# A two-layer hybrid decoder on one core: the order of paired weight loads, the planner's urgency rule, fixed buffers for the residual rows, and the queue that stores one product's tiles

## The chip, the core and the metric

The kernel runs on one core of a Trainium2 chip. Times are device microseconds of one execution. The core's engines are TensorE (PE, matmuls; PEld are its weight loads), VectorE (DVE), ScalarE (ACT), GpSimd (POOL) and SyncE (SP, which only issues DMA transfers here). ACT and POOL can issue DMA transfers too, each from its own queue, in the order of the program. The comparison is of the median time of the kernel before with that of the changed kernel.

## What is computed

Two layers, each with one input projection, three groups of heads, a gate and one output projection. Cut to what matters:

```python
def hybrid_layer(x, mem, w_in, b_forget, w_mem_kv, w_out, ln_gain, ln_bias):
    h = jnp.einsum('bsd,dn->bsn', x, w_in)
    (fq, fk, fv, fg, f_logit, dq, dk, dv, dg, iq, ik, iw, mq, mg) = jnp.split(h, offsets, axis=-1)
    y_fox = fox_attention(...) * silu(fg)       # 6 heads, causal, with a forget bias
    y_dsa = dsa_attention(...) * silu(dg)       # 6 heads, each query on its best 128 keys
    y_mem = memory_attention(...) * silu(mg)    # 4 heads on 256 memory tokens
    y = jnp.einsum('bsn,nd->bsd', jnp.concatenate([y_fox, y_dsa, y_mem], -1), w_out)
    return layer_norm(ALPHA * x + y, ln_gain, ln_bias)
```

The sequence has 512 rows, the model 2048 columns, a head 128; all inputs are float32. Every float32 operand is split into a high part (`whi`, `xh`, `qh`) and a low part (`wlo`, `xl`, `ql`), and a product is three matmuls: high x high, high x low, low x high.

## The kernel before

**Weights.** `stream()` lists the weights as chunks of 128 x 2048 float32 (1 MB), each worked on in two halves. The large projections are computed in blocks with seven products instead of eight (`P1`, `P7`, `Q4`, `P2`, `Q6`, `Q5`, `Q3`), so some right operands are sums of two weight blocks. Some of these sums are made in DRAM (by POOL, `weight_sums`), some by an accumulating load (`grow_w`) or on VectorE (`make_w`), and the operand T3 of P7 in pairs 1 to 5 is of the kind "pair": both blocks are loaded, one into `raw` and one, in four pieces of 256 KB, into slots called `other`, and `pair_w` adds them on VectorE. A layer has 10 such chunks.

For half n, the loop loads chunk i + 2 (`load_w`, on SP's queue), splits half n + 3 (ScalarE copies the high part, VectorE subtracts for the low part), adds the pair of half n + 4, and then issues the 12 matmuls of half n. `raw` has 7 buffers, the split weights (`whi`, `wlo`) 4, and nearly everything else, `other`, `z`, `row`, `vraw` and `halves` too, shares one pool of 69 slots.

**Stages of a layer.** Memory keys and values, then the indexer's chunks (iq), then the value products (`vs`: P1, P7, P2, Q6, Q4 for six pairs of column blocks, with early chunks for queries and keys between them), then Q5 and Q3 of the six pairs, during which the attention heads run, then the output projection.

**Side work.** What does not belong to a chunk is a generator. `begin(gen, wait)` puts it on a list, and `tick()` moves each on by a step; a yielded number is the count of ticks until its next step. A generator started with whole=True is moved twice a chunk in the indexer and once a chunk in the value products. `residual_rows` is one of them. In layer 1 it turns the normalised rows that layer 0 left in DRAM (x1) into layer 1's residual: for 12 tiles of 128 x 512 it loads the tile, multiplies by the gain and adds the bias (two VectorE operations; gain and bias rows are loaded by `load_row`, L1454), and stores the tile back from POOL's queue; the loads are on SP's queue (L1518). It takes a new slot for every tile and row. Its last step for a tile waits for `idle_dve(1.5)`: the planned VectorE at most 1.5 us behind TensorE.

**The planner.** While the kernel is written out, `Clock` keeps an estimated time for PE, ACT, DVE and POOL, charged for every operation. The heads are flows: generators that yield the engine of their next step. After each group of matmuls `advance()` picks, among the flows whose step `fits()`, the one with the lowest age, so the order in every engine's queue is fixed by it. Splits for Q5 and Q3 are flows as well (`split_steps`), with a due time of DUE = 10 us after they begin; one that is due within URGENT = 5 us goes ahead of all others, and `finish_flow` forces it out when its half is reached. An ACT or DVE step fits only if that engine is planned less than 1.5 us (heads) or 4 us (before) behind.

**Stores.** `val_out` takes a finished product out of PSUM. P2 of pair 0 is copied by ScalarE and stored with `store_v` (DMA `v<-vraw`); P2 of the pairs 1 to 5 is copied by ScalarE with its 16-bit halves interleaved (`halves`) and stored with `store_turned` (`vt<-halves`). Each is stored a tick later, two tiles a pair, from POOL's queue, as are all others of these stores. POOL's queue also holds the sums of weights, each behind a small operation (`seen<-mark`) that waits for ScalarE or VectorE.

Of the kernel before, what the change touches and what calls it, by code (L numbers as in the profile page):

```python
# [16 lines left out]
ALU = mybir.AluOpType  # L17
AX = mybir.AxisListType

P = 128  # L20
DM = 2048
# [15 lines left out]
SOON, LATER, URGENT, DUE = 1.5, 4.0, 5.0, 10.0  # L37
# [220 lines left out]
def kernel(  # L258
# [13 lines left out]
    clock = Clock()  # L272
    nc = Engines(tc.nc, clock)
# [11 lines left out]
    def uid(name):  # L285
        count[0] += 1
        return f"{name}_{count[0]}"
# [3 lines left out]
    def slot(name, dt=F32, w=512):  # L291
        t = slots.tile([P, w], dt, tag="s", name=uid(name))
        if name in COUNTED:
            out_now.append(t)
        return t
# [56 lines left out]
    def half(src, h):  # L352
        return src[:, h * H:(h + 1) * H]

    def load_w(i, pieces=2, some=(0, 1)):
        if i < len(chunks) and chunks[i][4][0] != "grown":
            kind, key = chunks[i][4]
            src = {"wall": lambda: wall[key], "sum": lambda: sums[key],
                   "pair": lambda: wall[key[0]]}[kind]()
            if chunks[i][0] == "out" and chunks[i][2][0] == "P7":  # L360
                for h in some:
                    t = [slot("grown") for _ in range(2)]
                    raw.setdefault(i, []).append(t)
                    for c in range(2):
                        nc.sync.dma_start(t[c], half(src, h)[:, c * 512:(c + 1) * 512])
                return
            w = DM // pieces
            for c in range(pieces):
                if c * 2 // pieces not in some:
                    continue  # L370
                if c * 2 % pieces == 0:
                    raw.setdefault(i, []).append(raws.tile([P, H], F32, tag="raw", name=uid("raw")))
                nc.sync.dma_start(raw[i][-1][:, c * w % H:c * w % H + w], src[:, c * w:(c + 1) * w])
                if i < 3 and c * 2 % pieces == 0:
                    load_mem(2 * i + c * 2 // pieces)
                if kind == "pair":
                    for e in (2 * c, 2 * c + 1):
                        t = others[i, e] = slot("other")
                        nc.sync.dma_start(t, wall[key[1]][:, e * 512:(e + 1) * 512])

    others = {}

    def pair_w(n):

# [220 lines left out]
    x1_d = dram.tile([SEQ, DM], F32, name="x1")  # L605
# [7 lines left out]
    def begin(gen, wait=0, last=False, whole=False, but=None):  # L613


        active.append([wait, gen, last, whole, but])
# [29 lines left out]
    def step_flow(f):  # L646

        eng = f[2]
        clock.floor = f[0]
        banks["held"] += f[3]  # L650
        try:
            need = next(f[1])
        except StopIteration:
            flows.remove(f)
            need = None
        clock.floor = 0.0
        done = clock.at[eng] + ahead[eng] if eng else clock.at["PE"]
        if need:
            f[2], f[3], floor, f[4] = (*need, None, None, None)[:4]
            f[3] = f[3] or 0  # L660
            f[0] = max(done, floor or 0.0)
# [14 lines left out]
    def advance():  # L676

        while flows:
            t = clock.at["PE"]
            freed[:] = [x for x in freed if x > t]  # L680
            room = 8 - banks["main"] - banks["held"] - len(freed)
            some = [f for f in flows if fits(f, room)]
            if not some:
                return
            step_flow(min(some, key=lambda f: f[5] if f[6] > t + URGENT else -1.0))

    def drain(done):

# [594 lines left out]
    def val_out(name, pair, st, ps):  # L1283

        j = 2 * pair
        m1, m7 = ("M1", pair, st), ("M7", pair, st)
        if name == "P2" and j in ROWS:
            d = slot("vraw")
            nc.scalar.activation(d, ps, AF.Copy)
            begin(store_v(d, (j, st)), 1)  # L1290
        elif name in ("P1", "P7"):
            d = vraw[m1 if name == "P1" else m7] = slot("vraw")
            nc.scalar.activation(d, ps, AF.Copy)
        elif name == "P2":
            begin(store_turned(halves(ps), (j, st)), 1)
        elif name == "Q6":
            d, e = slot("vraw"), vraw.pop(m7)
            nc.vector.scalar_tensor_tensor(d, ps, -1.0, vraw[m1], op0=ALU.mult,
                                           op1=ALU.subtract)
            nc.vector.tensor_tensor(e, e, d, op=ALU.add)  # L1300
            begin(store_v(d, (j + 1, 2 + st)), 1)
            begin(store_v(e, (j + 1, st)), 1)
        elif name == "Q4":
            d = vraw.pop(m1)
            nc.vector.tensor_tensor(d, d, ps, op=ALU.add)
            begin((store_v if j in ROWS else store_sum)(d, (j, 2 + st)), 1)
        elif j + 1 in ROWS:
            d = slot("vraw")
            nc.scalar.activation(d, ps, AF.Copy)
            begin(store_v(d, (j + 1, st + 2 * (name == "Q5")), True), 1)  # L1310
        else:
            d = vraw.pop(("base", name, pair, st))
            nc.vector.tensor_tensor(d, d, ps, op=ALU.add)
            begin(store_sum(d, (j + 1, st + 2 * (name == "Q5"))))
# [16 lines left out]
        return all(stored.get((j, st)) == 1 + j % 2 and stored_at[j, st] + LAND <= clock.at["PE"]  # L1331
                   for st in range(4))

    def store_v(t, key, add=False):
        note(key)
        j, st = key
        to = v_d[j][st * P:(st + 1) * P, :]
        if add:
            nc.gpsimd.dma_start(to, t, accum_op=ALU.add)
        else:  # L1340
            nc.gpsimd.dma_start(to, t)
        yield 1

    def load_head(key, j, c):
# [7 lines left out]
    def halves(t):  # L1352

        u = slot("halves", U16, 1024)
        nc.scalar.activation(u.rearrange("p (h e c) -> p h e c", h=4, e=2),
                             t.bitcast(U16).rearrange("p (h c e) -> p h e c", h=4, e=2), AF.Copy)
        return u

    def store_turned(u, key):
        note(key)  # L1360
        j, st = key
        to = vt_d[j].rearrange("h (s e) c -> s h e c", e=2)[st * P:(st + 1) * P]
        nc.gpsimd.dma_start(to.rearrange("s h e c -> s h (e c)"),
                            u.rearrange("p (h w) -> p h w", h=4))
        yield 1

# [68 lines left out]
    z, stats = {}, {}  # L1435
# [13 lines left out]
    rows = {}  # L1449

    def load_row(l, c, eng):
        for name, src in (("g", gain), ("b", bias)):
            t = rows[name, c] = slot("row")
            eng.dma_start(t, bass.AP(tensor=src.tensor, offset=src.offset + l * DM + c * 512,  # L1454
                                     ap=[[0, P], [1, 512]]))
# [42 lines left out]
    def scale_row(t, c, eng=nc.vector):  # L1498
        eng.tensor_tensor(t, t, rows["g", c], op=ALU.mult)
        eng.tensor_tensor(t, t, rows["b", c], op=ALU.add)  # L1500

    def residual_rows(l):

        tiles = [(st, c) for c in range(3) for st in range(4)]
        t, scaled = {}, None
        for n in range(len(tiles) + 1):
            if n:
                st, c = tiles[n - 1]
                scaled = (st, c, t.pop(n - 1))
                scale_row(scaled[2], c)  # L1510
                if st == 3:
                    del rows["g", c], rows["b", c]
            if n < len(tiles):
                st, c = tiles[n]
                if st == 0:
                    load_row(l - 1, c, nc.sync)
                t[n] = slot("z")
                nc.sync.dma_start(t[n], x1_d[st * P:(st + 1) * P, c * 512:(c + 1) * 512])  # L1518
            yield 1
            while not idle_dve(1.5):  # L1520
                yield 1
            if scaled:
                st, c, d = scaled
                nc.gpsimd.dma_start(x1_d[st * P:(st + 1) * P, c * 512:(c + 1) * 512], d)
                scaled = d = None
            yield 2

    terms = {}
# [72 lines left out]
    for i, (kind, l, j, col, _) in enumerate(chunks):  # L1601
        late = last_half(i)
        if kind == "out":
            step = OUT_ORDER.index(j)
            name, pair = j
# [13 lines left out]
        elif kind == "vs":  # L1619
            name, pair = j  # L1620
# [11 lines left out]
        else:  # L1632
            ps = bank("c")
        for h in range(2):
            n = 2 * i + h
# [27 lines left out]
            if kind == "out" and late:  # L1663
# [6 lines left out]
                if len(kept) == 16:  # L1670
# [3 lines left out]
                    for c in (0, 256):  # L1674
                        ps = bank("z")
                        c = slice(c, c + 256)
# [21 lines left out]
            elif kind == "mv":  # L1698
                for m in range(2):
                    for nn in range(2):  # L1700
                        k = 4 * col + 2 * h + nn
                        c = (k % 2) * 256 + m * P
# [3 lines left out]
            elif kind == "mk":  # L1706
                for kk in range(8):
                    k = 8 * h + kk
                    m = memT[k // 2]
                    c = (k % 2) * 256  # L1710
# [12 lines left out]
        if kind == "mk":  # L1723
            t = slot("kmem", F32R)
# [19 lines left out]
        elif kind == "small":  # L1744
# [4 lines left out]
            t = index_rope(ps, 64, 0, nc.vector)  # L1749
            kh2, kl2 = slot("kh2", F32R), slot("kl2", F32R)  # L1750
            for r in (0, 64):
                nc.scalar.activation(kh2[r:r + 64], t[:64], AF.Copy)
                nc.vector.tensor_tensor(kl2[r:r + 64], t[:64], kh2.bitcast(F32)[:64],
                                        op=ALU.subtract)
# [3 lines left out]
        elif kind == "iq":  # L1758
            t = index_rope(ps, P, P, nc.vector)
# [137 lines left out]
```

## Time and profile before

| | |
|---|---|
| median of 3 runs | 1895.98 us (1894.26 to 1899.74) |
| the profiled execution | 1893.36 us, of which the span from first to last instruction is 1891.5 us |
| mean granted TensorE clock | 0.996 |
| DMA moved | 478.39 MB, a mean of 253 GB/s |

The profile is of one execution. Its first part gives each engine's busy time, a fourth part the chain of work that ended last, and further views give the busy time of each engine in a stretch, what each engine waited for, and the instructions in order of time. A line of the timeline reads: start in us, duration in us, engine, line, operation, what is written <- what is read, shape, count, and in brackets the idle time before it and what ended it. SPq, POOLq and ACTq are the issuing sides of these engines. Nearly all compute operations are recorded under L242, the helper that calls them, so tiles tell them apart. A busy TensorE is not TensorE at its peak, since matmuls overlap: their starts lie closer than they are long.

### The profile page before, as it was taken

How to read it: one execution, taken by the hardware profiler on the slowest of the kernel's cores; microseconds unless marked ns; L12 is line 12 of the kernel's file. 1: busy time of each engine (PE TensorE's matmuls, PEld its weight loads, DVE VectorE, ACT ScalarE, POOL GpSimd, SP SyncE). 2: the span in 40 equal slices, each digit the busy share in tenths (PEclk: the TensorE clock that was granted, in tenths of full speed). 3: DMA queues.
4: the chain of work that ended last, by engine and by line, in shares of the span. 5: the costliest groups of instructions: out<-in, count | busy, mean ns of one | idle time of the engine just before them, and what ended most of it. 6: DMA issues, size and time to landing. Idle time of an engine off the chain costs nothing.

```text
span 1891.5 us, 26426 instructions
## 1 busy us (share of the span) xinstructions
PE 1856.0 (98%) x8994; PEld 1574.5 (83%) x8994; DVE 1610.3 (85%) x2565; ACT 1079.3 (57%) x1752; POOL 405.9 (21%) x595
## 2 busy tenths in 40 slices
PE   9999999999999999999999999999999999999997
PEld 8998888887887888888899977878778878888886
DVE  6789789888789997888887997898797889878798
ACT  5776344445457887555476653444353578875553
POOL 0111222122133311230021121221221333112302
PEclk9999999999999999999999999999999999999999
DMA  9986998898999888886598879988979998888866
GB/s 349 295 238 162 298 304 241 299 278 275 250 244 283 234 234 213 261 204 214 178 315 251 228 208 304 332 269 277 287 269 249 250 275 234 233 227 254 238 217 145
DMA packets 232164, 478.39 MB, mean 253 GB/s; under 512 B 76624, under 2 KB 101200, under 8 KB 231772
## 3 DMA queue, kind: packets, MB, share of 16 engines
q1 hardware_dynamic: 177660, 302.58, 49.9%
q0 software_dynamic: 53792, 173.06, 35.4%
q8 instruction: 71, 1.16, 0.2%
q10 hardware_dynamic: 576, 1.05, 0.1%
q14 instruction: 65, 0.53, 0.1%
HBM read 404.24 MB, written 152.07 MB: 294 GB/s over the span
## 4 chain that ended last, share of the span: by engine, by line
PE 80%; DVE 8%; DMA 5%; ACT 4%; issue 3%; POOL 0%; SPq 0%; DVEq 0%; ACTq 0%; POOLq 0%
PE v L242 39%; PE c L242 18%; PE z L242 15%; DVE wlo L242 3%; PE po L242 3%; DMA other<-in_wall_dram 2%; PE s L242 2%; DMA raw<-in_wall_dram 2%; ACT whi L242 2%; PE ix L242 2%; DVE raw L242 1%; PE pt L242 1%; ACT bt L242 1%; DVE acc L242 1%; PE sm L242 1%
## 5 line engine op out<-in xcount | busy, mean ns | idle before, releaser
L242 ACT ACTIVATE whi<-raw 128x1024 fp32r<-128x1024 f32 (+1 forms) x497 | 520.9, 1055 | 494.1 <-PE v L242 190.6
L242 DVE TENSOR_TENSOR wlo<-raw,whi 128x1024 fp32r<-128x1024 f32 (+1 forms) x497 | 601.2, 1217 | 118.8 <-ACT whi L242 116.5
L242 PE MATMUL v<-wlo,vxh 128*128 128x512 f32 x768 | 302.0, 393 | 12.1 <-DVE wlo L242 12.1
L242 PE MATMUL v<-whi,vxh 128*128 128x512 f32 x768 | 307.0, 400 | 6.3 <-ACT whi L242 3.7
L242 PE MATMUL v<-whi,vxl 128*128 128x512 f32 x768 | 301.0, 392 | 0.0
L242 PE MATMUL v<-wlo,xh 128*128 128x512 f32 x576 | 224.2, 389 | 0.2 <-DVE wlo L242 0.2
L242 PE MATMUL v<-whi,xh 128*128 128x512 f32 x576 | 224.2, 389 | 0.0
L242 PE MATMUL v<-whi,xl 128*128 128x512 f32 x576 | 224.2, 389 | 0.0
L242 PE MATMUL c<-xh,whi 128*128 128x512 f32 (+1 forms) x544 | 197.9, 364 | 0.0
L242 PE MATMUL c<-xh,wlo 128*128 128x512 f32 (+1 forms) x544 | 197.8, 364 | 0.0
L242 PE MATMUL c<-xl,whi 128*128 128x512 f32 (+1 forms) x544 | 197.7, 363 | 0.0
L242 POOL TENSOR_TENSOR seen<-mark,mhalf 128x1 f32<-128x1 f32 x88 | 47.9, 545 | 636.1 <-ACT mark L242 447.7
L242 PEld LDWEIGHTS v<-wlo,vxh 128*128 128x128 f32 x768 | 145.3, 189 | 44.4 <-DVE wlo L242 17.5
L242 PEld LDWEIGHTS v<-whi,vxh 128*128 128x128 f32 x768 | 145.0, 189 | 38.9 <-ACT whi L242 6.4
L242 PEld LDWEIGHTS v<-whi,vxl 128*128 128x128 f32 x768 | 144.9, 189 | 30.8
L242 PE MATMUL z<-wlo,yh 128*128 128x512 f32 (+1 forms) x434 | 168.1, 387 | 1.5 <-DVE wlo L242 1.5
L242 PE MATMUL z<-whi,yh 128*128 128x512 f32 (+1 forms) x434 | 168.7, 389 | 0.0
L242 PE MATMUL z<-whi,yl 128*128 128x512 f32 (+1 forms) x434 | 167.8, 387 | 0.0
L242 PEld LDWEIGHTS v<-wlo,xh 128*128 128x128 f32 x576 | 108.1, 188 | 23.1 <-DVE wlo L242 0.6
L242 PEld LDWEIGHTS v<-whi,xl 128*128 128x128 f32 x576 | 108.1, 188 | 22.6
L242 PEld LDWEIGHTS v<-whi,xh 128*128 128x128 f32 x576 | 108.1, 188 | 22.4
L242 PEld LDWEIGHTS c<-xl,whi 128*128 128x128 f32 x544 | 102.1, 188 | 12.2
(209 smaller groups left out, 3462.3 us busy)
## 6 DMA issues: line engine op xcount, KB each, us to landing
raw<-in_wall_dram SPq DMA_DIRECT2D x331, 512.0 KB, 7.4
sum<-in_wall_dram POOLq DMA_DIRECT2D x88, 1024.0 KB, 10.3
raw<-sum SPq DMA_DIRECT2D x72, 512.0 KB, 7.5
v<-vraw POOLq DMA_DIRECT2D x88, 256.0 KB, 8.3
other<-in_wall_dram SPq DMA_DIRECT2D x80, 256.0 KB, 14.1
vt<-halves POOLq DMA_DIRECT2D x56, 256.0 KB, 9.1
vraw<-v SPq DMA_DIRECT2D x56, 256.0 KB, 4.5
grown<-in_wall_dram POOLq DMA_DIRECT2D x48, 256.0 KB, 8.7
```

The lines of the kernel that those rows point to most:

```text
L242: return f(*args, **kw)
```

## The change

Four edits.

1. `load_w`: in each half of a pair chunk the two `other` pieces are issued ahead of `raw` instead of behind it.
2. `advance()`: a flow is urgent if it is due within URGENT plus the planned backlog of ACT and of DVE.
3. `residual_rows`: two tile buffers and two row buffers are held for the whole run and used in turn. The next tile is loaded at the start of a step, or behind the store where a new row of gain and bias begins; the two VectorE operations are issued after `idle_dve(1.5)`, the store a tick after them, and the next step two ticks after that.
4. `val_out`: the stores of P2 are issued from ScalarE's queue. The planner charges ACT 0.6 us for each, instead of POOL.

```diff
@@ load_w
+                if kind == "pair":
+                    for e in (2 * c, 2 * c + 1):
+                        t = others[i, e] = slot("other")
+                        nc.sync.dma_start(t, wall[key[1]][:, e * 512:(e + 1) * 512])
                 if c * 2 % pieces == 0:
                     raw.setdefault(i, []).append(raws.tile([P, H], F32, tag="raw", name=uid("raw")))
                 nc.sync.dma_start(raw[i][-1][:, c * w % H:c * w % H + w], src[:, c * w:(c + 1) * w])
                 if i < 3 and c * 2 % pieces == 0:
                     load_mem(2 * i + c * 2 // pieces)
-                if kind == "pair":
-                    for e in (2 * c, 2 * c + 1):
-                        t = others[i, e] = slot("other")
-                        nc.sync.dma_start(t, wall[key[1]][:, e * 512:(e + 1) * 512])
@@ advance
-            step_flow(min(some, key=lambda f: f[5] if f[6] > t + URGENT else -1.0))
+            near = t + URGENT + sum(max(clock.at[e] - t, 0.0) for e in ("ACT", "DVE"))
+            step_flow(min(some, key=lambda f: f[5] if f[6] > near else -1.0))
@@ val_out
-            begin(store_v(d, (j, st)), 1)
+            begin(store_v(d, (j, st), by=nc.scalar), 1)
...
-            begin(store_turned(halves(ps), (j, st)), 1)
+            begin(store_turned(halves(ps), (j, st), nc.scalar), 1)
@@ residual_rows
         tiles = [(st, c) for c in range(3) for st in range(4)]
-        t, scaled = {}, None
-        for n in range(len(tiles) + 1):
-            if n:
-                st, c = tiles[n - 1]
-                scaled = (st, c, t.pop(n - 1))
-                scale_row(scaled[2], c)
-                if st == 3:
-                    del rows["g", c], rows["b", c]
-            if n < len(tiles):
-                st, c = tiles[n]
-                if st == 0:
-                    load_row(l - 1, c, nc.sync)
-                t[n] = slot("z")
-                nc.sync.dma_start(t[n], x1_d[st * P:(st + 1) * P, c * 512:(c + 1) * 512])
-            yield 1
+        ring = [slot("z"), slot("z")]
+        row = [slot("row"), slot("row")]
+
+        def load(n):
+            st, c = tiles[n]
+            if st == 0:
+                for t, src in zip(row, (gain, bias)):
+                    nc.sync.dma_start(t, bass.AP(tensor=src.tensor,
+                                                 offset=src.offset + (l - 1) * DM + c * 512,
+                                                 ap=[[0, P], [1, 512]]))
+            nc.sync.dma_start(ring[n % 2], x1_d[st * P:(st + 1) * P, c * 512:(c + 1) * 512])
+
+        load(0)
+        for n, (st, c) in enumerate(tiles):
+            if st and n + 1 < len(tiles) and tiles[n + 1][0]:
+                load(n + 1)
+            yield 2
             while not idle_dve(1.5):
                 yield 1
-            if scaled:
-                st, c, d = scaled
-                nc.gpsimd.dma_start(x1_d[st * P:(st + 1) * P, c * 512:(c + 1) * 512], d)
-                scaled = d = None
+            d = ring[n % 2]
+            nc.vector.tensor_tensor(d, d, row[0], op=ALU.mult)
+            nc.vector.tensor_tensor(d, d, row[1], op=ALU.add)
+            yield 1
+            nc.gpsimd.dma_start(x1_d[st * P:(st + 1) * P, c * 512:(c + 1) * 512], d)
+            if n + 1 < len(tiles) and (not st or not tiles[n + 1][0]):
+                load(n + 1)
             yield 2
```

`store_v` and `store_turned` get an argument for the queue, with POOL's as the default.

More of the change, by code (lines that the diff above doesn't have):

```diff
@@ L353, in half @@
         return src[:, h * H:(h + 1) * H]
+    others = {}
     def load_w(i, pieces=2, some=(0, 1)):
@@ L375, in load_w @@
                     load_mem(2 * i + c * 2 // pieces)
-                if kind == "pair":
-                    for e in (2 * c, 2 * c + 1):
-                        t = others[i, e] = slot("other")
-                        nc.sync.dma_start(t, wall[key[1]][:, e * 512:(e + 1) * 512])
-    others = {}
     def pair_w(n):
@@ L1332, in kept_by, with store_v @@
                    for st in range(4))
-    def store_v(t, key, add=False):
+    def store_v(t, key, add=False, by=None):
         note(key)
@@ L1340, in store_v @@
         else:
-            nc.gpsimd.dma_start(to, t)
+            (by or nc.gpsimd).dma_start(to, t)
         yield 1
@@ L1357, in halves, with store_turned @@
         return u
-    def store_turned(u, key):
+    def store_turned(u, key, by=nc.gpsimd):
         note(key)
@@ L1362, in store_turned @@
         to = vt_d[j].rearrange("h (s e) c -> s h e c", e=2)[st * P:(st + 1) * P]
-        nc.gpsimd.dma_start(to.rearrange("s h e c -> s h (e c)"),
+        by.dma_start(to.rearrange("s h e c -> s h (e c)"),
                             u.rearrange("p (h w) -> p h w", h=4))
```

## The prediction

> **What bounds the kernel now.** I read the page's first and fourth part, then the busy times by stage, then what TensorE (PE) waited for in each stage, and last the timelines round its longest waits.
>
> ```profile
> PE 1856.0 (98%) x8994; PEld 1574.5 (83%) x8994; DVE 1610.3 (85%) x2565; ACT 1079.3 (57%) x1752; POOL 405.9 (21%) x595
> ...
> PE 80%; DVE 8%; DMA 5%; ACT 4%; issue 3%; POOL 0%; SPq 0%; DVEq 0%; ACTq 0%; POOLq 0%
> ```
>
> TensorE is idle for 1891.5 - 1856.0 = 35.5 us of the span, and the change adds or removes no matmul. So only those idle microseconds, and matmuls that run at a lower clock, can be won. The next view is busy time by stage: the value products of layer 0 (143:555) and layer 1 (1088:1500), and the heads of layer 0 (555:765) and layer 1 (1500:1709).
>
> ```profile
> 143.00:555.00 412.00, 409.49 (x1809) 338.26 (x1808) 350.27 (x484) 194.75 (x252) 94.57 (x144) 1.00 0.87 262
> 555.00:765.00 210.00, 206.64 (x1063) 175.10 (x1062) 182.68 (x344) 161.38 (x329) 50.48 (x63) 0.99 0.89 246
> ...
> 1088.00:1500.00 412.00, 402.67 (x1762) 329.02 (x1761) 351.26 (x490) 186.84 (x238) 95.21 (x153) 1.00 0.89 272
> 1500.00:1709.00 209.00, 205.62 (x1059) 174.26 (x1058) 181.62 (x343) 160.36 (x328) 49.05 (x62) 0.99 0.91 248
> ```
>
> After the length come the busy times of PE, PEld, DVE, ACT and POOL, then the clock and the DMA share. PE idles 2.5 us in the value stage of layer 0 and 9.3 us in that of layer 1, 6.8 us more for the same products. The heads cost 3.4 us of idle time in each layer. VectorE (DVE) is busy for 85% of both value stages, so its work has little room to be late. These four stages hold 18.6 of the 35.5 us; the rest is start, end and output projection, which the change leaves alone.
>
> **Part one: the urgency rule.** The longest wait of the heads is this one (timelines of PE, ACT and DVE; in brackets the idle time before the instruction, and what ended it):
>
> ```profile
> 584.01 0.53 PE L242 MATMUL v<-wlo,vxh 128*128 128x512 f32 x1 [2.14 <-DVE wlo L242]
> ...
> 578.56 1.04 ACT L242 ACTIVATE whi<-raw 128x1024 fp32r<-128x1024 f32 x1
> ...
> 579.70 2.39 DVE L242 TENSOR_TENSOR rope<-vraw,tabs 128x512 f32<-128x512 f32 x3
> 582.13 0.69 DVE L242 TENSOR_TENSOR rope<-rope,rope 128x512 f32<-128x512 f32 x1
> 582.74 2.35 DVE L242 TENSOR_TENSOR wlo<-raw,whi 128x1024 fp32r<-128x1024 f32 x2
> ...
> 1528.67 0.50 PE L242 MATMUL v<-wlo,vxh 128*128 128x512 f32 x1 [2.13 <-DVE wlo L242]
> ```
>
> The high half of the split weight was ready at 578.56 + 1.04 = 579.60, but its low half, wlo, stood behind a rope of four DVE operations (579.70 to 582.74) that no matmul waited for yet. Layer 1 repeats it to 0.01 us. The edit adds the planner's backlog of ScalarE and VectorE to the 5 us of URGENT, so a split turns urgent earlier just where these engines are loaded. In `advance()` an ACT or DVE step is placed only while that engine is planned at most 1.5 us behind in the heads (4 before them), so the margin grows by some 2 to 5 us, one to four attention steps. That puts both steps of the split ahead of the rope: wlo, 1.2 us long, starts near 579.7 and ends near 581.0, before the wait began (584.01 - 2.14 = 581.87).
>
> The wait also costs clock:
>
> ```profile
> 584.00:588.00 4.00, 3.99 (x10) 3.11 (x11) 4.00 (x6) 1.38 (x2) 0.00 (x0) 0.57 0.97 201
> ...
> 1528.60:1533.00 4.40, 4.33 (x13) 3.37 (x14) 4.40 (x7) 1.63 (x3) 0.00 (x0) 0.64 0.80 169
> ```
>
> The granted clock behind it is 0.57 over 4.0 us and 0.64 over 4.4 us, a loss of 4.0 x 0.43 = 1.7 and 4.4 x 0.36 = 1.6 us. So the wait is worth 2.14 + 1.7 = 3.8 us in layer 0 and 3.7 in layer 1. The second wlo of the pair at 582.74 ends at 585.09; without the wait its matmul would be due about 12 x 0.227 us (302.0 us over 768 matmuls is 0.39 each, but their starts are 0.227 apart) after the first's, near 584.5, so I leave 0.6 us per layer: the gain is 3.8 + 3.7 - 1.2 = **6.3 us**. What is pushed back, the ropes and the quotients, is late next; I charge 0.5 us per layer for it, **+1.0**. Bounds: -7.5 (both waits gone) and +5, if displaced steps make PE wait instead; 1.2 us is the nearest row for that (the wait for DVE vraw below), twice in each layer.
>
> ```profile
> PE v L242 <- DVE vraw L242: 1.2, 1, 1.2
> ```
>
> The Trainium skill bears on the clock (TensorE: Matmul & The Clock Gate, section "Part 1: The HAM clock gate"): it gives the idle time that halves the clock as about 3.4 us. By that rule a 2.14 us wait would not lower it, and this part would be an estimated 2.14 + 2.13 - 1.2 = 3.1 us instead of 6.3. The two rows above disagree, so the sum goes by them.
>
> **Part two: the residual rows.** Only layer 1 runs `residual_rows`, which loads a tile of x1, scales it on DVE and stores it from GpSimd's queue (POOL). SyncE (SP) issues the loads in the same queue as the weights. What SP waited for, then its issues in one stretch:
>
> ```profile
> SPq L1518 <- DVE acc L242: 19.2, 1, 19.2
> SPq L1454 <- DVE rope L242: 16.6, 1, 16.6
> ...
> SPq L1518 <- DMA x<-z: 8.1, 1, 8.1
> SPq L1454 <- DMA x<-z: 6.7, 2, 5.9
> ...
> 1178.09 0.33 SPq L373 DMA_DIRECT2D raw<-in_wall_dram  x1
> 1178.52 0.47 SPq L1454 DMA_DIRECT2D row<-in_gain_dram  x1
> 1185.01 0.33 SPq L1454 DMA_DIRECT2D row<-in_bias_dram  x1
> 1193.47 0.33 SPq L1518 DMA_DIRECT2D z<-x  x1
> 1193.88 3.88 SPq L373 DMA_DIRECT2D raw<-in_wall_dram  x5
> ```
>
> No weight is issued from 1178.4 to 1193.9, 15.5 us, because rows and tile take slots of the common pool that other stores (x<-z) still read; then five are issued at once. About 40 us later the pair chunk of that stretch makes PE wait:
>
> ```profile
> 1238.70 0.50 PE L242 MATMUL v<-whi,vxh 128*128 128x512 f32 x1 [0.91 <-ACT whi L242]
> 1239.97 0.50 PE L242 MATMUL v<-wlo,vxh 128*128 128x512 f32 x1 [0.76 <-DVE wlo L242]
> ```
>
> The new version holds two tile and two row buffers for its whole run and emits the two DVE operations only when the planned DVE backlog is at most 1.5 us. Loads (12 of z, 6 of rows), stores (12) and DVE operations stay the same in number; a tile takes at least five ticks instead of three, each one chunk long here, so the same work is thinner. It adds a wait: the third and fourth load of each row group reuse the buffer of the tile two before, whose store was emitted two ticks earlier, some 2 x 5.45 = 10.9 us (24 matmuls of 0.227 a chunk). The tile's own view gives price and landing:
>
> ```profile
> L242 DVE TENSOR_TENSOR z<-z,row x20: 683/690/693, 1062.8 to 1268.7; 128x512 f32<-128x512 f32 x20
> ...
> DMA to landing us min/median/max: 4.2/9.6/18.5
> ```
>
> A median of 9.6 us fits within 10.9; the slow ones do not, and then weight loads queue behind the waiting z load. The 6.8 us by which layer 1 exceeds layer 0 is the natural size of this part, since the residual rows are the work that layer 0 does not have. The work is still there, thinner, so I take two thirds, **4.5 us**. Bounds: -6.8, and +5 where the new wait blocks as the old did (third rival).
>
> **Part three: the order of the pair loads.** 20 chunks add two weights on DVE, 80 loads called other. Now each half issues raw first, and raw must wait for one of seven buffers; the others wait behind it.
>
> ```profile
> 384.33 5.21 SPq L373 DMA_DIRECT2D raw<-in_wall_dram  x3
> 389.59 1.14 SPq L379 DMA_DIRECT2D other<-in_wall_dram  x2
> ...
> 415.14 0.69 DVE L242 TENSOR_TENSOR raw<-raw,other 128x512 f32<-128x512 f32 x1 [2.96 <-DMA other<-in_wall_dram]
> ...
> 430.71 0.50 PE L242 MATMUL v<-whi,vxh 128*128 128x512 f32 x1 [0.73 <-ACT whi L242]
> 432.01 0.50 PE L242 MATMUL v<-wlo,vxh 128*128 128x512 f32 x1 [0.80 <-DVE wlo L242]
> ```
>
> The third raw at 384.33 is issued last of its row, at 384.33 + 5.21 - 0.33 = 389.2; the two others could go some 3 us earlier. DVE later sat 2.96 us for an other, and PE waited 0.73 + 0.80 at the end of that pair. But now raw lands last, both additions wait for it, and the DMA share is 0.87 over the stage: the same bytes move. I take 0.5 us in each layer, **1.0 us**; bounds -3 and +2 (both pair waits gone, or an addition of 0.69 later at three pairs).
>
> **Part four: the stores of P2.** Twelve in each layer, 24 in all: 4 of v, 20 of vt.
>
> ```profile
> 0.73 0.89 ACTq L242 DMA_DIRECT2D memraw<-in_memt_dram  x2
> ...
> L242 POOL DMA_DIRECT2D vt<-halves x56: 750/769/1128, 258.6 to 1617.7; - x56
> ...
> vt<-halves POOLq DMA_DIRECT2D x56, 256.0 KB, 9.1
> ```
>
> The trace has no store from ACT; its nearest issue, two loads in 0.89 us, gives 0.45 each, 10.7 us in all on an ACT that is busy 194.75 of 412 us. POOL loses 24 x 0.77 = 18.5 us, and it is 21% busy. The data is ACT's own copy, made a tick earlier, so ACT waits for nothing new; queued behind the issue are weight splits. What hides it is ACT's idle time; uncovered, each would cost 0.45. I take **0**, bounds -1 and +2. The Trainium skill speaks against a gain (DMA: Bandwidth & Descriptors, "Issuing engines are not separate DMA queues"): another issuing engine saves only issue time. That is an estimated 0 here too; no run shows it yet.
>
> **The sum.** -6.3 + 1.0 - 4.5 - 1.0 + 0 = -10.8 us. The profiled execution took 1893.36 (span 1891.5 and 1.9 around it), so it would take 1882.6. The median of the runs, 1895.98, lies 2.6 above it; from there the sum gives **1885.2 us**.
>
> **The rivals.** (a) In the heads the wait only moves: ropes or quotients pushed back hold PE as long as wlo did. For it: DVE is busy 182.68 of 210 us there, and from 579.70 to 585.09 without a break. Against: all that is left behind wlo is at present early. Then only 5.5 us are won: 1890.5. (b) The change does not do what it says for the rows: waits for DVE and for stores stay in the SP queue, only elsewhere. Heads and pairs alone give -6.3: 1889.7. (c) Slower: the new z load waits in SP's queue for its own buffer's store. If landing takes 18.5 us instead of 9.6, as at worst now, SP stands 18.5 - 10.9 = 7.6 us in front of the weights, up to six times; the 15.5 us block above preceded 0.91 + 0.76 us of waits at one pair, and if each block meets a pair and costs 2 us, that is +12 against the -6.3 of the heads and part three's 1.0 with nothing from part two: +6, 1902. It decides from landings above 10.9 us by more than the lead of the weights, some two chunks.
>
> **How the numbers follow.** My forecast (1879 to 1890) has 0.56, (a) 0.18, (b) 0.14, (c) 0.12. 0.3% of 1896 is 5.7 us, about what a measurement of this kernel can tell from no change, so faster is below 1890.3 and slower above 1901.7. Faster: 0.56, plus half of (a) and two thirds of (b), less 0.07 for mishaps: 0.67. Slower: half of (c) and a little: 0.08. Same: 0.25. The range goes from all waits won in the heads (7.5), in part two (6.8) and most of part three's bound, some -17, to just above no change: 1879 to 1898.
>
> **What would show it.** The waits of 2.1 us and the clock of 0.57 behind them are gone in both heads stages. PE idles 4 to 6 us in 1088:1500 instead of 9.3. SP's waits on the residual loads fall below 50 us in sum, and the row of x<-z shows whether its own stores now hold it. The vt and v stores under ACT number 24. The forecast is wrong if PE's new waits in the heads name pt, po or vraw with 2 us each, or if layer 1's value stage idles 9 us or more.

## The result and the profile after

The changed kernel took 1907.12 us (median of eight runs, 1904.07 to 1913.16), the kernel before 1895.97 beside it (eight runs, 1890.35 to 1903.77). The ratio is 1.0059, with a 95% interval from 1.0043 to 1.0076: slower by 11 us, where 1885.2 was forecast. The profiled execution has a span of 1904.1 us.

First the engines and the chain of work that ended last, from the page of the changed kernel:

```profile
PE 1863.6 (98%) x8994; PEld 1577.5 (83%) x8994; DVE 1606.7 (84%) x2565; ACT 1078.4 (57%) x1752; POOL 384.4 (20%) x571
...
PE 63%; DVE 13%; DMA 12%; issue 6%; ACT 4%; SPq 1%; POOL 0%; ACTq 0%; DVEq 0%; POOLq 0%
```

The same 8994 matmuls take 7.6 us more busy time, and the mean granted clock is 0.993 instead of 0.996; PE is idle for 40.5 us instead of 35.5. In the chain DMA has grown from 5% to 12% and DVE from 8% to 13%. Busy time by stage of the changed kernel (columns as in the prediction):

```profile
143.00:555.00 412.00, 405.18 (x1775) 332.75 (x1774) 347.43 (x482) 190.91 (x248) 77.59 (x120) 1.00 0.87 259
555.00:765.00 210.00, 208.06 (x1070) 175.97 (x1069) 179.86 (x340) 161.33 (x327) 53.60 (x73) 1.00 0.90 242
...
1088.00:1500.00 412.00, 397.51 (x1708) 322.92 (x1707) 344.93 (x482) 178.55 (x229) 76.06 (x123) 0.98 0.87 266
1500.00:1709.00 209.00, 207.18 (x1064) 175.30 (x1063) 182.47 (x339) 158.32 (x310) 54.67 (x73) 1.00 0.90 239
```

Both heads stages gained: 1.9 and 1.8 us of idle time instead of 3.4 each, and the clock is 1.00. Both value stages lost: 6.8 us instead of 2.5 in layer 0, 14.5 instead of 9.3 in layer 1, there with the clock down to 0.98. What PE waited for in layer 1's value stage is the same pair of splits as before, only more often and longer:

```profile
PE v L242 <- DVE wlo L242: 7.7, 11, 1.6
PE v L242 <- ACT whi L242: 6.8, 6, 2.2
```

So the splits were late, and the question is what held their weights. SyncE's queue, which issues them, stood on these (stage 1088 to 1510; us in total, times, longest):

```profile
SPq L1516 <- DMA x<-z: 22.4, 3, 11.1
SPq L1513 <- DVE z L242: 22.2, 3, 12.5
SPq L376 <- DMA vt<-halves: 17.6, 2, 14.2
```

L1516 is the new tile load, L1513 the new row load. In this stretch of the kernel before, the residual loads stood 8.1 and 5.9 us for x<-z and not at all for DVE z. The third row is a weight load that stands until a store of P2 has landed. Standing alone is not the cost: in the indexer just ahead (945 to 1088 us) SP stood 52.8 us in two waits at the new tile load, and PE was busy for all 143 us there. One block followed through to PE, from the timelines of the changed kernel (SP, POOL, DVE, then PE):

```profile
1193.96 0.33 SPq L379 DMA_DIRECT2D raw<-in_wall_dram  x1
1205.47 0.33 SPq L1516 DMA_DIRECT2D z<-x  x1
1205.90 1.72 SPq L379 DMA_DIRECT2D raw<-in_wall_dram  x2
...
1220.20 0.33 SPq L379 DMA_DIRECT2D raw<-in_wall_dram  x1
...
1198.92 0.58 POOL L242 DMA_DIRECT2D x<-z  x1
...
1193.80 1.41 DVE L242 TENSOR_TENSOR z<-z,row 128x512 f32<-128x512 f32 x2
...
1237.92 1.29 DVE L242 TENSOR_TENSOR raw<-raw,other 128x512 f32<-128x512 f32 x2 [3.38 <-DMA raw<-in_wall_dram]
...
1244.46 1.29 DVE L242 TENSOR_TENSOR raw<-raw,other 128x512 f32<-128x512 f32 x2 [1.49 <-DMA raw<-in_wall_dram]
...
1247.01 1.23 DVE L242 TENSOR_TENSOR wlo<-raw,whi 128x1024 fp32r<-128x1024 f32 x1
...
1247.03 0.75 PE L242 MATMUL v<-whi,vxh 128*128 128x512 f32 x1 [2.23 <-ACT whi L242]
1248.29 0.80 PE L242 MATMUL v<-wlo,vxh 128*128 128x512 f32 x1 [0.51 <-DVE wlo L242]
```

SP came to the tile load at 1194.3, when VectorE had only just begun to scale the tile whose buffer the load reuses; its store was issued at 1198.92 and the load at 1205.47. Of these 11.1 us, 0.9 passed until the scaling ended, 3.7 until the store was issued (GpSimd's queue stood on a `seen<-mark` until 1197.1 and issued a weight sum first), and 6.5 until it had landed. Meanwhile no weight was issued. Some 35 us later VectorE stands for the raw of a pair chunk, 3.38 and 1.49 us, and PE for the split made from it, 2.23 and 0.51. The first of these raw loads was issued at 1220.20, late in the row of loads behind the block, and landed at 1237.90, 17.7 us later, where the median of such loads is 7.1. The clock goes with it (windows of the changed kernel):

```profile
1247.00:1252.00 5.00, 4.46 (x10) 3.22 (x11) 4.92 (x7) 4.43 (x7) 1.02 (x2) 0.51 0.25 77
...
1252.00:1256.00 4.00, 4.00 (x15) 3.23 (x14) 3.93 (x5) 1.54 (x2) 0.00 (x0) 0.76 0.42 166
```

At this one pair chunk 2.23 + 0.51 = 2.7 us are idle, and 5.0 x 0.49 + 4.0 x 0.24 = 3.4 us go to the clock. At the same chunk the kernel before waited 0.91 + 0.76 us (the prediction's rows), and its clock stayed at full speed.

### The profile page after: what moved, and what is told of

Same layout as the page of the kernel before. It is cut to its first block, busy times and chain, and to the rows that moved or that the text cites. A ratio compares the mean times of both kernels' runs of the same rounds, so it can differ in the third digit from the quotient of the medians.

```text
span 1904.1 us, 26443 instructions
## 1 busy us (share of the span) xinstructions
PE 1863.6 (98%) x8994; PEld 1577.5 (83%) x8994; DVE 1606.7 (84%) x2565; ACT 1078.4 (57%) x1752; POOL 384.4 (20%) x571
## 4 chain that ended last, share of the span: by engine, by line
PE 63%; DVE 13%; DMA 12%; issue 6%; ACT 4%; SPq 1%; POOL 0%; ACTq 0%; DVEq 0%; POOLq 0%
PE v L242 28%; PE c L242 16%; PE z L242 11%; DMA raw<-in_wall_dram 8%; DVE wlo L242 6%; PE po L242 3%; DVE raw L242 2%; ACT whi L242 2%; PE ix L242 2%; DMA vt<-halves 1%; PE s L242 1%; PE pt L242 1%; DVE acc L242 1%; DVE z L242 1%; ACT bt L242 1%
## 5 line engine op out<-in xcount | busy, mean ns | idle before, releaser
L242 PE MATMUL v<-wlo,vxh 128*128 128x512 f32 x768 | 304.7, 397 | 11.1 <-DVE wlo L242 11.1
L242 PEld LDWEIGHTS v<-whi,vxh 128*128 128x128 f32 x768 | 145.7, 190 | 48.9 <-ACT whi L242 15.6
L242 PEld LDWEIGHTS c<-xl,whi 128*128 128x128 f32 x544 | 102.1, 188 | 12.1
## 6 DMA issues: line engine op xcount, KB each, us to landing
sum<-in_wall_dram POOLq DMA_DIRECT2D x88, 1024.0 KB, 10.9
```

The source lines that it names most:

```text
L242: return f(*args, **kw)
```

## The experiments

Each was timed beside the kernel before, whose median lay between 1894.4 and 1897.1 us in the four groups of runs. Differences below are against the median of the same group; the intervals are those of the ratios.

**The parts one by one.** e1 and e2 divide the change at the stores, e3, e4 and e5 take the order of the pair loads, the urgency rule and the residual rows by themselves; their edits are those hunks of the diff.

> The kernel before with part four alone (P2's 24 stores from ScalarE's queue). Theory L (transfers in flight): in the trace of the changed kernel a load of SP often waits for a vt store of ScalarE to land, as if both queues drew on the same eight completion counters; two of eight are held for 16 to 27 us just when a pair's loads begin. Then this kernel is slower than before by 4 to 12 us, PE idles 5 to 7 us in 143:555 (2.5 before), and SP's waits there name the vt stores with 20 us or more. Theory O (the order of the pair loads, or the ring of the rows, is to blame): this kernel is within 2 us of before and its value stage idles 2.5 to 3.5 us.

> The changed kernel without part four: P2's stores back on GpSimd's queue, the other three parts kept. Theory L: faster than before by 5 to 11 us, with PE idle 2 to 3 us in 143:555. Theory O: slower than before by 3 us or more, with PE idle 6 us or more in 143:555 as in the changed kernel.

> The kernel before with part one of the diff alone (the two other pieces ahead of raw). Theory L: within 2 us of before, since the bytes and counters are the same. Theory O: slower by 4 us or more, with more idle time of PE at the pair chunks of both layers.

> The kernel before with the urgency rule alone. Both theories: the heads improve as in the changed kernel (idle 3.4 us to about 1.9 in each layer, no stretch of half clock) and the value stages stay as before, so 4 to 8 us faster. If it is not faster, the gain in the heads is given back later, in the output projection.

> The kernel before with the new residual rows and nothing else. By the runs so far the three without the stores are 9 us slower than before, the order alone is 4 us slower and the urgency alone 6 us faster, so this part should cost what is left: theory R (the new tile and row loads stand at the head of SP's queue and keep the weights behind them) says 8 to 12 us slower, that is 1904 to 1908, PE idle in layer 1's value stage (1088 to 1510 us) 14 us or more, and waits of SP of some 20 us each on x<-z and on DVE z at the two new load lines. Rival M (the parts only hurt together, through the order of the pair loads): 1894 to 1898, with layer 1 idling 9 to 10 us as before.

| kernel | us | against before | interval of the ratio |
|---|---|---|---|
| e1 stores alone | 1899.36 | +2.8 | 1.0008 to 1.0030 |
| e2 the other three | 1905.46 | +8.9 | 1.0038 to 1.0072 |
| e3 order alone | 1900.59 | +4.0 | 1.0017 to 1.0038 |
| e4 urgency alone | 1890.08 | -6.5 | 0.9959 to 0.9979 |
| e5 residual rows alone | 1911.14 | +15.6 | 1.0064 to 1.0113 |

Theory L, which put the loss on the stores, fell with e2: without them the kernel is still 8.9 us slower. Its sign on SP was there in e1 (waits of SP on the vt stores in the two value stages, of which the kernel before has none):

```profile
SPq L373 <- DMA vt<-halves: 31.0, 5, 8.9
...
SPq L373 <- DMA vt<-halves: 26.3, 4, 8.6
```

With the waits at L379 they are 36.2 and 41.5 us. But e1 lies below theory L's 4 to 12 us and above theory O's 2, and layer 0's value stage idles 2.3 us in its profile, not 5 to 7. That profiled execution, 1895.27 us, lies 4.1 below its median, so it doesn't show where the 2.8 us went. e5 lies above theory R's 8 to 12 us; rival M is out. The rows are the largest loss, by themselves larger than that of the whole change. The four alone add up to 2.8 + 4.0 - 6.5 + 15.6 = +15.9, together they cost 11.2; the intervals of the four leave room for this difference. Windows of e5 and what SP waited for in it:

```profile
1088.00:1500.00 412.00, 396.12 (x1698) 321.28 (x1697) 343.43 (x478) 177.26 (x226) 82.80 (x134) 0.98 0.86 265
```

```profile
SPq L1515 <- DMA x<-z: 25.0, 3, 12.3
...
SPq L1512 <- DVE z L242: 20.6, 3, 10.9
```

The loss sits in the one stage in which the rows run (15.9 us idle, clock 0.98), with the same two waits as in the changed kernel.

**Is it the waiting loads, or the place of the vector operations?** e6 leaves every buffer and operation of e5 and changes only the queue of the eighteen loads. e7 leaves them in SP's queue, but emits each only when its buffer should be free by the plan; e8 adds the urgency rule.

```diff
# e6, in load(): twice
-                    nc.sync.dma_start(
+                    nc.gpsimd.dma_start(
# e7, e8: ahead of load(n + 1) at the start of a step
+                while clock.at["PE"] < at[(n + 1) % 2] + 25.0:
+                    yield 1
# behind the store
+            at[n % 2] = clock.at["PE"]
# ahead of load(n + 1) behind the store
+                while clock.at["PE"] < at[n % 2 if st else 1 - n % 2] + 25.0:
+                    yield 1
```

> The new residual rows with the eighteen loads (rows and tiles) issued by GpSimd's queue instead of SyncE's; buffers, vector operations and the planned order of everything else stay as in the ring alone. Theory R (weights queued behind waiting loads): SP's queue never stands on x<-z or DVE z, the loss of the ring alone goes, time 1893 to 1898, idle time in layer 1's value stage back at 9 to 10 us; GpSimd's queue stands instead. Rival V (the loss comes from where the vector operations of the rows now fall between the weight splits): time within 2 us of the ring alone. Rival G (stores of v and vt behind the loads in GpSimd's queue come late and heads wait for them): slower again, waits in the heads.

> The new residual rows, loads still in SyncE's queue, but each load is emitted only when the planned clock stands 25 us past the store (or past the last use of the rows) that it must wait for, so that it finds its buffer free. Theory R: waits of SP on x<-z and DVE z at the two load lines fall under 5 us each in sum, time 1891 to 1897, idle time in layer 1's value stage 7 to 10 us. Rival V (place of the vector operations): the thinner rows move them once more, so any time from 1895 to 1908, and no relation to the SP waits.

> The urgency rule and the residual rows with the later loads; order of the pair loads and stores as before. Theory R with separate parts: the urgency's 6.5 us less than the run with later loads alone, 1885 to 1891, with the heads at 1.9 us of idle time each. If the parts of the change do not add up, it lies above 1893.

e6 took 1900.52 us (+5.0; 1.0005 to 1.0034), e7 1896.14 (+0.6; 0.9988 to 1.0019), e8 1896.90 (+1.3; 0.9988 to 1.0023). Moving the loads out of SP's queue takes away two thirds of the 15.6 us with nothing else changed, so that much comes from standing at the head of that queue; rival V, within 2 us of e5, has failed. It is 2.5 us above theory R's range, with 10.9 us of idle time in layer 1's value stage; GpSimd's queue now stands in its place (its waits in e6):

```profile
POOL z L242 <- DMA x<-z: 13.5, 2, 10.4
```

Emitting them later takes away all of it; at the new loads SP now stands only this long (its waits in e7; none for DVE z):

```profile
SPq L1516 <- DMA x<-z: 5.2, 1, 5.2
```

In the windows of e7 one stage gains and the next loses:

```profile
1088.00:1500.00 412.00, 406.99 (x1786) 335.05 (x1785) 354.31 (x494) 186.51 (x237) 94.27 (x152) 1.00 0.90 273
1500.00:1709.00 209.00, 202.08 (x1033) 171.39 (x1032) 180.57 (x343) 160.09 (x325) 49.22 (x62) 0.98 0.89 246
```

The value stage idles 5.0 us instead of 9.3, just what was forecast of the rows, but the heads idle 6.9 instead of 3.4: the last tile is scaled at 1528 us (timeline of e7), in the heads.

```profile
1528.44 1.41 DVE L242 TENSOR_TENSOR z<-z,row 128x512 f32<-128x512 f32 x2
```

That this tile makes the heads wait is not shown: the longest new wait there, 1.78 us of PE for DVE ql, ended at 1507.08, before it.

e8 did not show the gain of the urgency rule that was expected (1885 to 1891). Its last tile is scaled at 1519 us, in the heads too; but its profiled execution, 1890.60 us, lies 6.3 below its median, so the trace doesn't show where the median's time went, and that stays open.

**A shorter distance.** e9 and e10 are e7 and e8 with 14.0 in place of 25.0.

> The new residual rows alone, each load emitted 14 us of the planned clock after the store (or the last use of the rows) that it waits for, instead of 25. With 25 us layer 1's value stage fell to 5.0 us of idle time, but the last tile was scaled at 1529 us, inside the heads, whose idle time rose from 3.4 to 6.9. Theory R (head of SP's queue) plus lateness: a tile now takes some 34 us instead of 45, the last one is scaled near 1430 to 1460 inside the value stage, that stage idles 4 to 8 us, the heads 3.4 again, time 1889 to 1895. Rival V (any place of the rows' vector operations costs about as much): 1895 to 1900. If 14 us is too short for the landings, SP stands on x<-z again and the time is above 1900.

> The same with the urgency rule. If the gains add: 6 us less than the run without it, 1883 to 1889, below both kernels and below the urgency alone (1890.1). Rival S (with the urgency rule the displaced work is late wherever rows are still open): as with 25 us, 1894 to 1899.

e9 took 1895.73 (-1.3; 0.9982 to 1.0007), e10 1887.42 (-9.7; 0.9938 to 0.9969): faster than the kernel before and than the changed one. It is 3.2 us better than the urgency alone (-6.5), but the two lie in different groups and their intervals overlap, so that step is not clear of the noise. e9 lies 0.7 us above theory R's range and would suit rival V, which e6 had ruled out; e10 lies inside the range for gains that add. The last tile is scaled at 1450 us in e9, inside the value stage. The windows of e10:

```profile
555.00:765.00 210.00, 208.06 (x1078) 176.17 (x1077) 182.49 (x346) 163.18 (x330) 50.73 (x66) 1.00 0.90 245
...
1088.00:1500.00 412.00, 405.30 (x1770) 331.87 (x1769) 354.58 (x496) 185.15 (x236) 96.31 (x154) 1.00 0.90 272
1500.00:1709.00 209.00, 207.25 (x1077) 175.51 (x1076) 182.68 (x344) 165.12 (x334) 47.97 (x61) 1.00 0.92 250
```

The heads keep their gain in both layers, and layer 1's value stage idles 6.7 us instead of 9.3.

**The order of the pair loads.** VectorE's waits in the two value stages, first of the kernel before, then of e3 (layer 0, then layer 1):

```profile
DVE raw L242 <- DMA other<-in_wall_dram: 12.3, 7, 3.0
...
DVE raw L242 <- DMA other<-in_wall_dram: 22.6, 11, 3.2
```

```profile
DVE raw L242 <- DMA raw<-in_wall_dram: 12.2, 5, 4.4
...
DVE raw L242 <- DMA raw<-in_wall_dram: 24.5, 7, 5.9
```

The wait did not go, it changed its name: what is issued last lands last, and the sum goes from 34.9 to 36.7 us, in fewer and longer waits. In e3's profile PE idles 4.7 and 10.4 us in the two value stages instead of 2.5 and 9.3. In layer 0 one pair chunk makes up the loss; there the kernel before waited 0.73 and 0.80 us (the prediction's rows) at full clock (timeline and windows of e3):

```profile
433.00 0.79 PE L242 MATMUL v<-whi,vxh 128*128 128x512 f32 x1 [3.48 <-ACT whi L242]
...
434.00:438.00 4.00, 3.70 (x9) 2.96 (x10) 3.93 (x7) 3.44 (x6) 1.06 (x2) 0.50 0.34 80
```

So a sum of VectorE's waits hides what one long wait costs PE, in time and then in clock. e11 cuts raw in two, each half behind its own other:

```diff
                     for e in (2 * c, 2 * c + 1):
                         t = others[i, e] = slot("other")
                         nc.sync.dma_start(t, wall[key[1]][:, e * 512:(e + 1) * 512])
+                        nc.sync.dma_start(raw[i][-1][:, e % 2 * 512:e % 2 * 512 + 512],
+                                          src[:, e * 512:(e + 1) * 512])
+                    continue
```

> The order of the pair loads alone, but raw comes in two pieces of 256 KB, each behind its own other (other, raw piece, other, raw piece): the same bytes, 40 more transfers. Theory A (with the order turned, both additions wait for the whole 512 KB raw, which lands last; before, the first addition waited only for the first of the two others): the first addition starts after half of the bytes, the vector engine's wait on raw falls below the 12.2 and 24.5 us of the order alone, time 1894 to 1898 against 1900.6. Rival B (the others take common buffers earlier and SP stands longer for other reasons): stays at 1899 to 1903.

It took 1899.66 us (+2.6; 1.0007 to 1.0029), inside rival B's range, and not to be told from e3. VectorE's waits in e11:

```profile
DVE raw L242 <- DMA raw<-in_wall_dram: 14.3, 6, 3.7
...
DVE raw L242 <- DMA raw<-in_wall_dram: 29.0, 10, 5.6
```

They did not fall, they rose to 43.3 us, so theory A has failed. In e11's profile layer 0 idles 2.4 us as before, and layer 1 idles 11.2: the loss has changed its place. That the order costs some 4 us and gains nothing is shown; which load is late at which chunk, and why, stays open.

**The stores.** e12 to e14 leave P2's own stores on GpSimd's queue and put a store on ScalarE's queue beside each of the 20 vt stores, to a scratch place that nobody reads: 8 KB, then the whole tile in rows of 2 KB, then in rows of 512 bytes.

```diff
+        to = dram.tile([16, 256], U16, name=uid("side"))
+        nc.scalar.dma_start(to, u[0:16, 0:256])
...
+        to = dram.tile([P, 1024], U16, name=uid("side"))
+        nc.scalar.dma_start(to, u)
...
+        to = dram.tile([4, P, 256], U16, name=uid("side"))
+        nc.scalar.dma_start(to.rearrange("h s c -> s h c"), u.rearrange("p (h w) -> p h w", h=4))
```

> The kernel before, and beside each of the 20 vt stores of P2 on GpSimd's queue a store of 8 KB from ScalarE's queue to a scratch place: the issue time on ScalarE without the slow landing. Theory K (the 2.8 us that the stores alone cost come from transfers that land late on counters that SP's loads share): within 1.2 us of before, 1894.5 to 1897. Rival I (issue time on ScalarE, 20 x 0.38 = 7.6 us in front of weight splits): 1897.5 to 1900.

> As the tiny stores beside, but each of the 20 side stores is the whole 256 KB tile in rows of 2 KB (one piece per partition) from ScalarE's queue. It adds 5.2 MB to some 170 MB, and the landing time of a full tile on the counters that SP's loads share. Tiny stores left the time unchanged, so issue time is out. Theory K1 (any full-size store on these counters holds up SP's loads): 1898.5 to 1902, with SP waits on the side stores of over 20 us in sum. Theory K2 (only stores in short rows land late enough): within 1.5 us of before, side stores landing in about 9 us.

> The same side stores of 256 KB, written in rows of 512 bytes as the vt stores of the change are. Theory K2: landing about 16 us as for vt in the changed kernel, SP waits on the side stores of over 30 us in sum, time 2 us or more above the side stores in 2 KB rows, 1899 to 1903. Theory K1: the same as those within 1.5 us.

| kernel | us | against before | interval of the ratio | landing, us | SP waits on side stores, both value stages |
|---|---|---|---|---|---|
| e12, 8 KB | 1895.92 | -1.2 | 0.9984 to 1.0010 | 5.6 | 0.8 us |
| e13, 2 KB rows | 1901.52 | +7.1 | 1.0027 to 1.0053 | 10.1 | 7.5 us |
| e14, 512 B rows | 1906.49 | +12.1 | 1.0052 to 1.0076 | 16.5 | 86.9 us |

SP's waits in e14 that make up the last figure (layer 0's two rows, then layer 1's):

```profile
SPq L373 <- DMA side<-halves: 38.5, 5, 10.7
...
SPq L379 <- DMA side<-halves: 2.5, 1, 2.5
...
SPq L373 <- DMA side<-halves: 30.7, 4, 12.1
...
SPq L379 <- DMA side<-halves: 15.2, 2, 11.8
```

Issue time on ScalarE costs nothing that can be measured (e12). The row size by itself is worth 1906.49 - 1901.52 = 5.0 us, which puts e14 above both ranges, and with it come SP's waits. By the trace's semaphore events the transfers of SP and ScalarE take eight completion semaphores in turn, and a weight load whose turn falls on a store's stands until that store has landed. e13 fits neither theory whole: its time is K1's, its waits are K2's. It also moves 5.2 MB more than the kernel before, which the change does not, and how much of the 7.1 us is these bytes was not separated. So the numbers of e13 and e14 are no price for the change; that is e1's 2.8 us. What they share with the change is the landing (DMA issues of the changed kernel):

```profile
vt<-halves POOLq DMA_DIRECT2D x36, 256.0 KB, 6.6
...
vt<-halves ACTq DMA_DIRECT2D x20, 256.0 KB, 16.0
```

**The change with the rows repaired.** e15 is the changed kernel with the three edits of e9.

> The whole change with one repair: the loads of the residual rows are emitted 14 us of the planned clock after the store or last use that they wait for. Theory R: the ring's waiting loads are most of the change's loss. The repaired ring and the urgency gave 1887.4; the order of the pair loads (4 us alone) and the stores (2.8 us alone) come on top: 1892 to 1896, with layer 1's value stage idling 8 to 11 us instead of 14.5. If the order or the stores cost more in company than alone, it stays above 1899.

It took 1896.52 us (+2.1; 0.9991 to 1.0021), half a microsecond above the range for theory R. The change was +11.2 without this repair, so the waiting loads are some 9 us of it. Against e10's -9.7 it is 11.8 us up (9.1 by the two medians themselves, which lie in different groups): the order and the stores, 4.0 + 2.8 = 6.8 alone, may cost more in company, but the intervals leave room for the plain sum. The value stages carry the loss (windows of e15, whose profiled execution, 1901.07 us, lies 4.6 above its median; 12.2 us idle in layer 1, more than the 8 to 11 expected):

```profile
143.00:555.00 412.00, 406.33 (x1790) 334.68 (x1790) 348.81 (x483) 193.07 (x251) 80.22 (x124) 1.00 0.87 262
...
1088.00:1500.00 412.00, 399.77 (x1717) 326.09 (x1716) 347.83 (x485) 180.58 (x230) 76.57 (x126) 0.98 0.89 267
```

## Why the prediction was wrong

**Part one, the urgency rule: right.** Net -5.3 was forecast, e4 gave -6.5. The waits of 2.1 us and the half clock behind them are gone in both heads, and the new waits there are at most 0.6 us (waits of PE in the changed kernel, 555 to 765):

```profile
PE v L242 <- ACT vraw L242: 0.8, 2, 0.5
PE v L242 <- DVE vraw L242: 0.6, 1, 0.6
PE v L242 <- DVE rec L242: 0.5, 1, 0.5
```

The cause is the forecast one: the same low half now stands ahead of that rope (timeline of the changed kernel).

```profile
584.78 1.21 DVE L242 TENSOR_TENSOR wlo<-raw,whi 128x1024 fp32r<-128x1024 f32 x1
...
587.52 2.40 DVE L242 TENSOR_TENSOR rope<-vraw,tabs 128x512 f32<-128x512 f32 x3
```

Its high half was ready at 584.33, 0.45 us before; in the kernel before 3.14 us lay between.

Rival (a), a wait that only moves, was not seen.

**Part two, the residual rows: the step that failed.** It read: "whose store was emitted two ticks earlier, some 2 x 5.45 = 10.9 us", and "A median of 9.6 us fits within 10.9". The landing held in the block followed above (the store at 1198.92 had landed by the load's 1205.47, in 6.5 us), though the view's 9.6 us is a median over stores and loads of z together; the distance did not hold. Ticks are distance on the plan's clock, and SP's queue does not keep to it: it runs on until something holds it, and it came to the load 4.6 us before the store was issued, not 10.9 us after. The row loads, which wait for the vector operations emitted one tick before them, were not seen at all; they make up half of SP's 44.6 us in the value stage. -4.5 was forecast, alone it is +15.6. The sign that SP's waits on the residual loads fall below 50 us failed too: with the 52.8 us in the indexer they are over 97. Rival (c) had the place, loads that stand for their own buffer's store, and nearly the size: six blocks of 7.6 us are 45.6, at 2 us each +12. Part of that is luck: it put the waits on slow landings, which only one of the three blocks on x<-z shows (the store at 1283.17 let its load go at 1296.42, 13.2 us later), and the three waits on DVE z were not in it. It was given 0.12, on the strength of a median landing that was not what decided. The range, too, was drawn short of its 1902.

What was thought to be the gain is there, once the loads don't wait: layer 1's value stage idles 5.0 us in e7 and 6.7 in e10. e10, urgency and rows without order and stores, took 9.7 us off; the forecast for those two parts was -6.3 + 1.0 - 4.5 = -9.8. That this agrees is in part luck: the repaired rows alone gave +0.6 and -1.3 (e7, e9), neither to be told from nothing, so the 4.5 us were not shown as time.

**Part three, the order: wrong in sign.** -1.0 was forecast, +4.0 measured, beyond the bound of +2. The working had the reason itself: "now raw lands last, both additions wait for it". It still took 0.5 us a layer as a gain, because the others "could go some 3 us earlier". The step that failed is this gain against its own argument, and the bound: one later raw at one pair chunk cost 3.48 us of waiting and then clock (e3), where an addition of 0.69 us was allowed for.

**Part four, the stores: cover missed.** 0 was forecast with ACT's idle time as the cover and +2 as the upper bound; e1 gave +2.8. ScalarE's issue time is covered indeed (e12). What the working did not look at is SP: its weight loads wait for the landing of ScalarE's stores (77.7 us in e1's two value stages), and from the new queue these land later. That these waits are the 2.8 us fits e12 to e14, but it is not shown by itself: 86.9 us of them in e14 went with +12.1. The Trainium skill (DMA: Bandwidth & Descriptors, "Issuing engines are not separate DMA queues") says that another issuing engine saves only issue time. On the gain this case agrees: none was seen. That sentence does not speak of the loss: the same 20 stores landed in 16.7 us (median) from ScalarE's queue in e1 and in 10.1 from GpSimd's before.

## What to carry to other kernels

A planner's ticks say nothing of when a queue arrives at an instruction. For each load that is put into a queue with others behind it, look up what frees its buffer, and whether that is surely done when the queue gets there, not when the plan does; here loads emitted 14 us later on the plan were worth some 9 us of the whole change, and loads emitted 25 us later pushed the work into the next stage. Where two transfers are both needed, their order moves the wait from one name to the other; and moving stores to another queue asks how long they take to land from there and whose completion they share.

## What the runs showed of the hardware

- Stores of one tile in rows of 512 bytes landed in 16.0 to 16.7 us (median of 20) from ScalarE's queue; the same 20 stores landed in 10.1 from GpSimd's in the kernel before (9.1 is the median of all 56 vt stores there). With rows of 2 KB ScalarE's landed in 10.1. On the page the move took 1920 packets off GpSimd's queue and put 11136 on ScalarE's for the same 6.29 MB, 3.3 KB against 565 bytes each (queues of the changed kernel; before they had 53792 and 576 packets):

```profile
q0 software_dynamic: 51872, 166.77, 34.7%
q10 hardware_dynamic: 11712, 7.34, 1.3%
```

- Behind a PE wait of 2.23 us the granted clock was 0.51 over 5.0 us and 0.76 over the next 4.0 (changed kernel, 1247 to 1256 us). The Trainium skill (TensorE: Matmul & The Clock Gate, "Part 1: The HAM clock gate") gives some 3.4 us of idle time for that; this trace again shows a lower clock after less.
